# Modulation products in runs of two row tiles, spread by the columns of products done

## The chip, the core and the metric

The kernel runs on one core of one Trainium2 chip. The metric is device time of that core in microseconds, for one execution of the whole network. All operands are in HBM at the start; the output goes back there.

## The reference, cut to what matters

Two blocks follow each other on 256 tokens of width 1024. The first has four layers with two streams, latent tokens (256) and context tokens (256); the second has one layer with three attentions, a merge and a gated MLP, on the latent tokens alone. The change touches the first block only:

```python
def modulation(cvec, w_ada, b_ada):              # cvec: 1024; w_ada: 1024 x 3072
    return jnp.split(jax.nn.silu(cvec) @ w_ada + b_ada, 3, axis=-1)

for i in range(4):                               # mixers: window GQA, MLA, mLSTM, window GQA
    sh_l, sc_l, gt_l = modulation(c, w_ada, b_ada)
    sh_c, sc_c, gt_c = modulation(c_ctx, w_ada, b_ada)
    h_l = rmsnorm(x_lat, g_pre) * (1 + sc_l) + sh_l
    h_c = rmsnorm(x_ctx, g_pre) * (1 + sc_c) + sh_c
    y_l, y_c = mixer(h_l, h_c)                   # h @ w_in, attention, ... @ w_out
    x_lat = x_lat + gt_l * rmsnorm(y_l, g_post)
    x_ctx = x_ctx + gt_c * rmsnorm(y_c, g_post)  # not in the last layer
```

A layer's modulation depends on `c` and `c_ctx` only, so it can be computed at any time ahead of its use: shift and scale when the layer's input is normalised, the gate when its output is added.

## The kernel before

**Products.** An fp32 operand is held as two halves, high (`wh`, `thl`, ...) and low (`wl`, `tll`, ...), and every large product is three matmuls over them (`gemm_a`, L366 to L368, 512 columns at a time; `gemm_b`, L377 to L380, 256 columns). The weights come in parts of 512 KB (`load_part`): SP issues a DMA into one of three buffers `wr`, ScalarE makes the high half (L345) and VectorE the low half (L347).

**Modulation.** `c` and `c_ctx` stand side by side as two of 32 columns of `cs`. A block is 1024 of the 3072 output columns: block 0 and block 1 hold half the scale and half the shift each, block 2 the gate. One row tile is 128 rows of `w_ada` by the 1024 columns of a block, 512 KB, in one of two buffers `ar`; eight row tiles make a block. Per row tile four products (L518), one for each 256 columns, go to four groups of 32 columns of the array and to four groups of 32 partitions of one PSUM tile; in fp32 each is two instructions, so a row tile is eight. A block holds its PSUM tile, one of three of the tag `tp`, from its first product to its last. Then the columns are evacuated (L535), transposed (L712) and turned into the next layer's scale and shift, or, for the gate, multiplied and written to DRAM, from where they are read back across the partitions. Layer 0's own shift and scale are made ahead of everything by `ada_first` (L490).

**What is done when.** While layer l runs, its own gate (block 2) and layer l+1's blocks 0 and 1 are due: 24 row tiles in layers 0, 1 and 2, and 8 in layer 3. They are steps of a generator, `self.filler`: one step loads one row tile and multiplies it. The generator is stepped by `load_part`, once behind each weight part that is loaded (`pump(rate)`, L339; not in layer 0's first two input blocks), and run to a given point by `drain`: up to the gate ahead of the output projection, and to its end behind each stream of the output projection (L648). With about as many weight parts as row tiles in a layer, some steps are left to the output projection, whose eight parts pump too.

```python
            raw = self.raw(src, off, kc * n)
            self.pump(rate)
```

**Order.** The program is written in one order and the Tile scheduler makes each engine's queue from it: of the instructions that it believes ready it takes the one that stands first in the program. TensorE, ScalarE, VectorE and SP then take their queues strictly in order on the chip, so an instruction that the scheduler put too early holds all behind it. By this the products of later parts of the program stand between the steps of an attention (`tp` transposes at L910 and L1110, exponentials at L889, products with the values at L915 and L1118 to L1120), and eight instructions of one row tile need not stand together. The loads of `ar` wait on SP until the product that reads the buffer last is done, with the loads of `wr` behind them.

**Attention and banks.** PSUM tags have these banks: `mm` three (products), `S` two (scores), `tp` three (transposes, attention outputs, modulation). In `gqa` (layers 0 and 3) an attention output holds one `tp` bank over two heads' groups while the transposed probabilities of each key tile go through another and are copied out by ScalarE or VectorE in turn (L704, L708); layer 0 has 48 such groups of four transposes, 24 in each of its two calls of `attend`.

Of the kernel before, what the change touches and what calls it, by code (L numbers as in the profile page):

```python
# [19 lines left out]
F32 = mybir.dt.float32  # L20
# [3 lines left out]
AF = mybir.ActivationFunctionType  # L24
OP = mybir.AluOpType
# [7 lines left out]
WSZ = 512 * KS  # L33
NRAW = 3
NADA = 2
RATE = 1
NW = 5
NMID = 4
SLOTS = {"wfh": 2, "wfl": 2, "K8": 2, "Z4": 4, "Q4": 4, "P4": 4, "T2": 3, "V4": 1}
# [58 lines left out]
WEIGHTS = {}  # L98
# [170 lines left out]
class Net:  # L269
    def __init__(self, tc, A, out, stack, upto=99):  # L270
        self.tc, self.nc, self.A, self.out = tc, tc.nc, A, out
        self.upto = upto
        P = lambda name, bufs, **k: stack.enter_context(tc.tile_pool(name=name, bufs=bufs, **k))
        self.const = P("const", 1)
        self.res = P("res", 1)
        self.wp = P("wp", 2)
        self.tmp = P("tmp", 2)
        self.ps = P("ps", 2, space=PSUM)
        self.dram = P("dram", 1, space=bass.MemoryType.DRAM)
        self.open("act")  # L280
        self.flip = 0
        self.deep = 0
        self.filler = iter(())
        self.later = None
        self.n = 0

# [39 lines left out]
        return self.act.tile(shape, dt, name=self.nm(name), tag=name, bufs=1)  # L326


    def load(self, name, b, tags=None, rate=RATE):

        return [self.load_part(name, b, i, tags, rate) for i in range(len(WEIGHTS[name].off[b]))]

    def load_part(self, name, b, i, tags=None, rate=RATE):
        nc, w = self.nc, WEIGHTS[name]
        src = self.A["w_" + name]
        if True:
            off, k0, kc, n = w.off[b][i]
            raw = self.raw(src, off, kc * n)
            self.pump(rate)  # L339
            if tags is None:  # L340
                hi = self.wp.tile([128, WSZ], F32R, name=self.nm("wh"), tag="w", bufs=2 * NW)
                lo = self.wp.tile([128, WSZ], F32R, name=self.nm("wl"), tag="w", bufs=2 * NW)
            else:
                hi, lo = (self.t([128, WSZ], F32R, t) for t in tags)
            nc.scalar.activation(hi[:, :kc * n], raw[:, :kc * n], AF.Copy)  # L345
# [13 lines left out]
    def gemm_a(self, ps, xh, xl, parts, KC=8, n0=0, n=None):  # L359

        n = n or ps.shape[-1]
        nc = self.nc
        for k0, kc, wh, wl in parts:
            for k in range(kc):
                kk = k0 + k
                nc.tensor.matmul(ps, xh(kk), wh[:, k, n0:n0 + n], start=kk == 0, stop=False)  # L366
                nc.tensor.matmul(ps, xh(kk), wl[:, k, n0:n0 + n], start=False, stop=False)  # L367
                nc.tensor.matmul(ps, xl(kk), wh[:, k, n0:n0 + n], start=False, stop=kk == KC - 1)  # L368

    def gemm_b(self, outs, parts, n0, KC=8, m=128):  # L370

        nc = self.nc
        for k0, kc, wh, wl in parts:
            for k in range(kc):
                kk = k0 + k
                for ps, xh, xl in outs:
                    nc.tensor.matmul(ps, wh[:, k, n0:n0 + m], xh(kk), start=kk == 0, stop=False)  # L377
                    nc.tensor.matmul(ps, wh[:, k, n0:n0 + m], xl(kk), start=False, stop=False)  # L378
                for ps, xh, xl in outs:
                    nc.tensor.matmul(ps, wl[:, k, n0:n0 + m], xh(kk), start=False, stop=kk == KC - 1)  # L380


    def dma(self, out, in_):
# [79 lines left out]
                "l": l, "bcol": bcol, "gpre": gpre,  # L463
                "g": self.dram.tile([2, D], F32, name=f"gate{l}")}

    def pump(self, n):
        for _ in range(n):
            if next(self.filler, None) is None:
                break

    def drain(self, upto=None):

        for v in self.filler:
            if upto is not None and v == upto:
                break

    def ada_first(self, mod, g):
# [24 lines left out]
            nc.vector.tensor_mul(mod["A"][v][:, ks], t, gpre[:, ks])  # L502
            nc.vector.tensor_add(mod["B"][v][:, ks], tp[:, 2:4, j], bcol[:, ks])

    def ada_steps(self, mod, pairs):


        nc, A = self.nc, self.A
        l, bcol, gpre = mod["l"], mod["bcol"], mod["gpre"]
        w = WEIGHTS[f"l{l}_ada"]  # L510
        src = A[f"w_l{l}_ada"]
        for b in pairs:
            ps = self.pt([128, 256], "tp")
            for off, k, kc, n in w.off[0 if l == 0 else b]:
                r = self.wp.tile([128, 1024], F32, name=self.nm("ar"), tag="ar", bufs=NADA)
                self.dma(r, bass.AP(tensor=src.tensor, offset=src.offset + off, ap=[[n, 128], [1, n]]))
                for g in range(4):
                    nc.tensor.matmul(ps[32 * g:32 * g + 32, :], self.cs[:, k, :], r[:, g * 256:(g + 1) * 256],  # L518
                                     start=k == 0, stop=k == 7)
                yield "part"  # L520
            rows = self.mid([128, 256])
            if b == 2:
                br = self.tmp.tile([128, 2, 256], F32, name=self.nm("br"), tag="big", bufs=2)
                for i, t in enumerate(("brow", "gpost")):
                    for g in range(4):
                        self.dma(br[32 * g:32 * g + 32, i], bass.AP(tensor=A[f"l{l}_{t}"].tensor,
                                                                    offset=A[f"l{l}_{t}"].offset + g * 256,
                                                                    ap=[[0, 32], [1, 256]]))
                nc.vector.tensor_add(rows, ps, br[:, 0])
                nc.vector.tensor_mul(rows, rows, br[:, 1])  # L530
                for g in range(4):
                    self.dma(mod["g"][:, g * 256:(g + 1) * 256], rows[32 * g:32 * g + 2, :])
                yield "gate"
                continue
            nc.scalar.activation(rows, ps, AF.Copy)  # L535
            tp = self.pt([128, 2, 128], "tp")
            self.transposes(tp, rows, 2)
            cp = tp.rearrange("p j (h g v) -> p h g j v", h=2, g=2)
            pair = lambda x: x.rearrange("p (g j) -> p g j", g=2)
            k0 = b * 4  # L540
            for i, v in enumerate("lc"):
                t = self.tmp.tile([128, 4], F32, name=self.nm("sc"), tag="sc", bufs=2)
                nc.vector.scalar_tensor_tensor(pair(t), cp[:, 0, :, :, i], 1.0, pair(bcol[:, 8 + k0:12 + k0]),
                                               op0=OP.add, op1=OP.add)
                nc.vector.tensor_mul(mod["A"][v][:, k0:k0 + 4], t, gpre[:, k0:k0 + 4])
                nc.vector.tensor_add(pair(mod["B"][v][:, k0:k0 + 4]), cp[:, 1, :, :, i], pair(bcol[:, k0:k0 + 4]))

    def ada_all(self, mod, nxt):
        yield from self.ada_steps(mod, (2,))
        if nxt is not None:  # L550
            yield from self.ada_steps(nxt, (0, 1))

    def gates(self, mod, streams):

# [220 lines left out]
    def gqa(self, l, hT, mod, nxt, need_ctx, p0):  # L775
# [68 lines left out]
            return lambda q, i, b: lq[q][:, i, b, :]  # L844

        p0 = p0 or self.load(name, 0)
        p1 = self.load(name, 1, ("Z4", "P4"), rate=0 if l == 0 else RATE)
        q0 = {}
        if l == 0:
            for s, q, tag in (("c", 0, "mm"), ("c", 1, "mm"), ("l", 0, "mm"), ("l", 1, "S")):  # L850
# [80 lines left out]
            for g, z in enumerate((z0, z1)):  # L931
                self.split(y, g, z, qstreams)
        if need_ctx:
            self.drain("gate")
        else:
            self.drain()
            self.constants()
# [4 lines left out]
    def mla(self, hT, mod, nxt):  # L942
# [192 lines left out]
        y = self.halves("cl")  # L1135
        for g in range(2):
            self.split(y, g, z[g], "cl")
        self.drain("gate")
        self.mark("out1")
        return self.out_proj("l1_out", "cl", y, mod, nxt)  # L1140

# [1 line left out]
    def mlstm(self, hT, mod, nxt):  # L1143
# [233 lines left out]
        self.drain("gate")  # L1377
        self.mark("out2")
        return self.out_proj("l2_out", "lc", y, mod, nxt)

# [579 lines left out]
    def run(self):  # L1960
# [8 lines left out]
        for g in range(4):  # L1969
            self.ada_first(mod, g)  # L1970
            self.turn(hT["c"], xn["c"], *AB["c"], (g,))
            p0.append(self.load_part("l0_in", 0, g, None, 0))
# [55 lines left out]
```

## Time and profile before

| what | us |
|---|---|
| median of 3 runs | 1478.16 (1475.01 to 1479.94) |
| the profiled execution, its own time | 1472.61 |
| its span, first to last instruction | 1470.8 |
| TensorE matmul busy | 1433.8 (97% of the span) |
| TensorE weight load busy | 1171.0 (80%) |
| VectorE busy | 1046.3 (71%) |
| ScalarE busy | 737.2 (50%) |
| mean granted TensorE clock | 0.996 of full speed |

The four layers of the first block take roughly the first 960 us, the second block the rest. PE is the matmul side of TensorE, PEld its weight loads, DVE VectorE, ACT ScalarE, SP the engine that issues the DMAs. Matmuls overlap in the array, so the duration of one (0.28 us for 256 columns) is longer than the distance to the next.

### The profile page before, as it was taken

The numbers are of one execution on the slowest core, as the hardware profiler recorded it, in microseconds if no ns is written. First come the engines' busy times: TensorE is split into PE (matmuls) and PEld (weight loads), VectorE is DVE, ScalarE is ACT, GpSimd is POOL, SyncE is SP. The second block draws the span as 40 slices with busy tenths as digits, with TensorE's granted clock in tenths as the row PEclk, the third lists the DMA queues.
The fourth block names the chain that finished last, engine by engine and source line by source line (L and its number), as shares of the span: only waits on it lengthen the run. The fifth ranks groups of instructions, "written<-read, shape, count | busy, mean of one in ns | idle before, by whom it ended". The sixth has DMA issues, their size and how long they took to land.

```text
span 1470.8 us, 24541 instructions
## 1 busy us (share of the span) xinstructions
PE 1433.8 (97%) x9445; PEld 1171.0 (80%) x9445; DVE 1046.3 (71%) x2241; ACT 737.2 (50%) x1447; POOL 50.3 (3%) x72
## 2 busy tenths in 40 slices
PE   7999999999899999999999999999999999899998
PEld 4876677779687777787878777768988899799987
DVE  4678765553687666696585768889787887799963
ACT  4555543442456344364544535656575645466542
POOL 0000000000000000010000000000000000211100
PEclk9999999999999999999999999999999999999999
DMA  9601315552313325424323332246524444555552
GB/s 364 199 1 58 115 63 202 202 193 94 122 44 110 134 72 179 158 72 163 110 101 115 128 131 100 88 127 216 176 98 158 154 133 134 182 186 186 183 178 98
DMA packets 63555, 203.35 MB, mean 138 GB/s; under 512 B 10329, under 2 KB 14542, under 8 KB 63438
## 3 DMA queue, kind: packets, MB, share of 16 engines
q1 hardware_dynamic: 63438, 201.79, 40.8%
q8 instruction: 74, 1.21, 0.3%
q14 instruction: 43, 0.35, 0.1%
HBM read 200.65 MB, written 1.11 MB: 137 GB/s over the span
## 4 chain that ended last, share of the span: by engine, by line
PE 86%; DMA 5%; DVE 5%; ACT 2%; issue 1%; POOL 0%; SPq 0%; ACTq 0%; DVEq 0%; POOLq 0%
PE mm L366 11%; PE mm L368 11%; PE mm L367 11%; PE mm L377 8%; PE mm L378 7%; PE mm L380 7%; DMA ar<-in_w_l_ada_dram 3%; PE tp L518 3%; PE tp L915 3%; PE tp L910 3%; PE tp L712 2%; PE S L876 1%; PE S L380 1%; PE S L377 1%; PE S L378 1%
## 5 line engine op out<-in xcount | busy, mean ns | idle before, releaser
L347 DVE TENSOR_TENSOR wl<-wr,wh 128x1024 fp32r<-128x1024 f32 (+5 forms) x168 | 196.9, 1181 | 68.5 <-ACT wh L345 66.0
L345 ACT ACTIVATE wh<-wr 128x1024 fp32r<-128x1024 f32 (+5 forms) x172 | 174.6, 1026 | 90.6 <-PE mm L378 32.8
L377 PE MATMUL mm<-thl,wh 128*128 128x256 f32 x608 | 175.3, 289 | 1.3 <-ACT thl L661 1.3
L378 PE MATMUL mm<-tll,wh 128*128 128x256 f32 x608 | 173.5, 286 | 0.0
L380 PE MATMUL mm<-thl,wl 128*128 128x256 f32 x608 | 173.2, 286 | 0.0
L366 PE MATMUL mm<-wh,thl 128*128 128x512 f32 (+3 forms) x312 | 122.6, 393 | 1.4 <-ACT thl L661 1.0
L367 PE MATMUL mm<-wl,thl 128*128 128x512 f32 (+3 forms) x312 | 122.2, 392 | 0.0
L368 PE MATMUL mm<-wh,tll 128*128 128x512 f32 (+3 forms) x312 | 122.2, 392 | 0.0
L377 PEld LDWEIGHTS mm<-thl,wh 128*128 128x128 f32 x608 | 116.2, 191 | 4.2 <-issue 1.9
L378 PEld LDWEIGHTS mm<-tll,wh 128*128 128x128 f32 x608 | 116.3, 191 | 1.6 <-issue 1.2
L380 PEld LDWEIGHTS mm<-thl,wl 128*128 128x128 f32 x608 | 116.0, 191 | 0.7 <-issue 0.3
L368 PE MATMUL mm<-wh,tlc 128*128 128x512 f32 (+2 forms) x240 | 94.0, 394 | 0.3 <-DVE tlc L1886 0.3
L366 PE MATMUL mm<-wh,thc 128*128 128x512 f32 (+2 forms) x232 | 92.6, 399 | 1.6 <-DVE thc L595 1.6
L367 PE MATMUL mm<-wl,thc 128*128 128x512 f32 (+2 forms) x232 | 91.1, 394 | 0.0
L347 DVE TENSOR_TENSOR wl<-wrd,wh 128x1024 fp32r<-128x1024 f32 x52 | 65.9, 1269 | 27.5 <-ACT wh L345 27.4
L889 ACT ACTIVATE P<-S,nm 128x512 f32<-128x512 f32 (+1 forms) x96 | 58.6, 614 | 53.3 <-DVE nm L882 45.4
L366 PEld LDWEIGHTS mm<-wh,thl 128*128 128x128 f32 x312 | 58.7, 188 | 13.0 <-issue 1.6
L368 PEld LDWEIGHTS mm<-wh,tll 128*128 128x128 f32 x312 | 58.7, 188 | 10.8 <-issue 1.0
L345 ACT ACTIVATE wh<-wrd 128x1024 fp32r<-128x1024 f32 x52 | 53.6, 1050 | 26.6 <-PE mm L367 23.7
L367 PEld LDWEIGHTS mm<-wl,thl 128*128 128x128 f32 x312 | 58.7, 188 | 10.0 <-issue 0.8
L377 PE MATMUL mm<-thc,wh 128*128 128x256 f32 (+1 forms) x216 | 65.5, 303 | 0.1
L380 PE MATMUL mm<-thc,wl 128*128 128x256 f32 (+1 forms) x216 | 64.8, 300 | 0.0
(564 smaller groups left out, 3744.9 us busy)
## 6 DMA issues: line engine op xcount, KB each, us to landing
ar<-in_w_l_ada_dram SPq DMA_DIRECT2D x80, 512.0 KB
wr<-in_w_l_in_dram SPq DMA_DIRECT2D x48, 512.0 KB
wr<-in_w_l_out_dram SPq DMA_DIRECT2D x32, 512.0 KB
wr<-in_w_s_mg_dram SPq DMA_DIRECT2D x24, 512.0 KB
wrd<-in_w_s_down_dram SPq DMA_DIRECT2D x22, 512.0 KB
wrd<-in_w_s_gate_dram SPq DMA_DIRECT2D x20, 512.0 KB
wrd<-in_w_s_up_dram SPq DMA_DIRECT2D x20, 512.0 KB
wr<-in_w_s_br_dram SPq DMA_DIRECT2D x12, 512.0 KB
```

The costliest lines, as they stand in the source:

```text
L345: nc.scalar.activation(hi[:, :kc * n], raw[:, :kc * n], AF.Copy)
L347: eng.tensor_sub(lo[:, :kc * n], raw[:, :kc * n], hi[:, :kc * n].bitcast(F32))
L366: nc.tensor.matmul(ps, xh(kk), wh[:, k, n0:n0 + n], start=kk == 0, stop=False)
L367: nc.tensor.matmul(ps, xh(kk), wl[:, k, n0:n0 + n], start=False, stop=False)
L368: nc.tensor.matmul(ps, xl(kk), wh[:, k, n0:n0 + n], start=False, stop=kk == KC - 1)
L377: nc.tensor.matmul(ps, wh[:, k, n0:n0 + m], xh(kk), start=kk == 0, stop=False)
L378: nc.tensor.matmul(ps, wh[:, k, n0:n0 + m], xl(kk), start=False, stop=False)
L380: nc.tensor.matmul(ps, wl[:, k, n0:n0 + m], xh(kk), start=False, stop=kk == KC - 1)
L518: nc.tensor.matmul(ps[32 * g:32 * g + 32, :], self.cs[:, k, :], r[:, g * 256:(g + 1) * 256], start=k == 0, stop=k == 7)
L889: nc.scalar.activation(p[:, :nk], ps[:, i, :], AF.Exp, scale=scale, bias=nm[:, r:r + 1], accum_out=sm[:, r:r + 1])
L910: nc.tensor.transpose(tp[:, r, :], P[r][:, j * 128:(j + 1) * 128], self.eye)
L915: nc.tensor.matmul(o[i * 64:(i + 1) * 64, kv], vv, pT[:, 2 * i:2 * i + 2, :], start=j == 0, stop=j == nj - 1)
```

## The change

Three things change together. A step of the generator now takes two row tiles: it first sends the product of the pair that the step before has fetched, and then fetches the next pair into the two buffers; the first pair of a layer is fetched at the layer's start. The sixteen instructions of a pair are sent as one run: the first waits for the tile fetched last, and the others are tied to stand behind it in TensorE's queue, with high priority. And the generator is no longer stepped by weight parts, but by `earn`: each `gemm_a` or `gemm_b` adds the columns it has sent to a credit, and when the credit reaches the layer's pace (19000, 16000, 29000, 24000 columns) one step is taken. `drain(mod)` steps until the gate is done. By these columns the twelve steps of layers 0 to 2 end ahead of the output projection, at some 233,000 of 344,000 columns in layer 0, 194,000 of 301,000 in layer 1 and 356,000 of 492,000 in layer 2; the four of layer 3 end at 98,000. Shapes, loads and arithmetic stay what they are; the two row tiles of a pair are added in the other order.

```diff
-RATE = 1
+PACE = (19000, 16000, 29000, 24000)
...
+        self.pace = self.credit = 0
...
     def load_part(self, name, b, i, tags=None):
             raw = self.raw(src, off, kc * n)
-            self.pump(rate)
...
     def gemm_a(...)
+        self.earn(3 * n * sum(p[1] for p in parts))
...
     def gemm_b(...)
+        self.earn(sum(3 * o[0].shape[-1] for o in outs) * sum(p[1] for p in parts))
+
+    def earn(self, columns):
+        self.credit += columns
+        if self.credit >= self.pace > 0:
+            self.credit -= self.pace
+            next(self.filler, None)
...
-    def pump(self, n):
-        for _ in range(n):
+    def drain(self, gate=None):
+        for _ in iter(lambda: gate is not None and "done" in gate, True):
             if next(self.filler, None) is None:
-                break
-
-    def drain(self, upto=None):
-        for v in self.filler:
-            if upto is not None and v == upto:
                 break
...
-    def ada_steps(self, mod, pairs):
-        for b in pairs:
-            ps = self.pt([128, 256], "tp")
-            for off, k, kc, n in w.off[0 if l == 0 else b]:
-                r = self.wp.tile([128, 1024], F32, name=self.nm("ar"), tag="ar", bufs=NADA)
-                self.dma(r, bass.AP(tensor=src.tensor, offset=src.offset + off, ap=[[n, 128], [1, n]]))
-                for g in range(4):
-                    nc.tensor.matmul(ps[32 * g:32 * g + 32, :], self.cs[:, k, :], r[:, g * 256:(g + 1) * 256],
-                                     start=k == 0, stop=k == 7)
-                yield "part"
+    def ada_steps(self, blocks):
+        todo = None
+        for mod, b in blocks:
+            l = mod["l"]
+            parts = WEIGHTS[f"l{l}_ada"].off[0 if l == 0 else b]
+            src = A[f"w_l{l}_ada"]
+            for i in range(0, len(parts), NADA):
+                if todo is not None:
+                    self.ada_product(*todo)
+                rows = []
+                for off, k, kc, n in parts[i:i + NADA]:
+                    r = self.wp.tile([128, 1024], F32, name=self.nm("ar"), tag="ar", bufs=NADA)
+                    self.dma(r, bass.AP(tensor=src.tensor, offset=src.offset + off, ap=[[n, 128], [1, n]]))
+                    rows.insert(0, (k, r))
+                todo = (mod, b, rows)
+                yield True
+        self.ada_product(*todo)
+        yield True
+
+    def ada_product(self, mod, b, rows):
+        k0 = min(k for k, _ in rows)
+        if k0 == 0:
+            mod["ps"] = self.pt([128, 256], "tp")
+        ps = mod["ps"]
+        def part(i, g):
+            k, r = rows[i]
+            return self.nc.tensor.matmul(ps[32 * g:32 * g + 32, :], self.cs[:, k, :], r[:, g * 256:(g + 1) * 256],
+                                         start=k0 == 0 and i == 0, stop=k0 + NADA == 8 and i == NADA - 1)
+        self.together([(lambda i=i, g=g: part(i, g)) for i in range(NADA) for g in range(4)])
+        if k0 + NADA == 8:
+            (self.ada_gate if b == 2 else self.ada_columns)(mod, b, ps)
+
+    def together(self, work):
+        first = work[0]()
+        with self.tc.issue_after(first.ins), self.tc.high_priority():
+            for w in work[1:]:
+                w()
...
-        p1 = self.load(name, 1, ("Z4", "P4"), rate=0 if l == 0 else RATE)
+        p1 = self.load(name, 1, ("Z4", "P4"))
...
-            self.filler = self.ada_all(mod, nxt)
+            self.filler = self.ada_steps([(mod, 2)] + ([(nxt, 0), (nxt, 1)] if nxt is not None else []))
+            self.pace, self.credit = PACE[l], 0
+            next(self.filler)
```

`ada_gate` and `ada_columns` hold the former code for a finished block, moved and otherwise unchanged; `ada_gate` marks the gate as done.

## Rows read from the trace of the kernel before

**Rows 1.** The page's busy shares: busy us, share of the span, instructions.

```profile
PE 1433.8 (97%) x9445; PEld 1171.0 (80%) x9445; DVE 1046.3 (71%) x2241; ACT 737.2 (50%) x1447; POOL 50.3 (3%) x72
```

**Rows 2.** Table by stretches: length, busy us of engines, clock, DMA share, GB/s.

```profile
145.00:215.00 70.00, 69.94 (x512) 47.30 (x510) 49.51 (x128) 35.57 (x94) 0.00 (x0) 1.00 0.23 77
215.00:240.00 25.00, 24.22 (x211) 22.90 (x210) 10.90 (x15) 6.68 (x8) 0.00 (x0) 1.00 0.46 166
382.00:384.00 2.00, 2.00 (x11) 0.99 (x12) 1.36 (x5) 0.00 (x0) 0.00 (x0) 0.50 0.13 52
```

**Rows 3.** Instructions grouped by line, L518: busy us, mean ns, idle before, releaser.

```profile
L518 PE MATMUL tp<-ar,cs 128*32 128x256 f32 x640 | 57.3, 398 | 7.1 <-DMA ar<-in_w_l_ada_dram 7.0
```

**Rows 4.** Timeline of PE around a run of 8: start us, duration us, instruction.

```profile
247.46 0.40 PE L366 MATMUL mm<-wh,thc 128*128 128x512 f32 x1
247.70 0.39 PE L367 MATMUL mm<-wl,thc 128*128 128x512 f32 x1
248.01 0.64 PE L518 MATMUL tp<-ar,cs 128*32 128x256 f32 x8
248.58 0.50 PE L368 MATMUL mm<-wh,tlc 128*128 128x512 f32 x1
248.92 0.39 PE L366 MATMUL mm<-wh,thc 128*128 128x512 f32 x1
```

**Rows 5.** Timeline of PE around a run of 16.

```profile
240.02 0.28 PE L378 MATMUL mm<-tll,wh 128*128 128x256 f32 x1
240.14 0.28 PE L380 MATMUL mm<-thl,wl 128*128 128x256 f32 x1
240.35 1.07 PE L518 MATMUL tp<-ar,cs 128*32 128x256 f32 x16
241.35 0.50 PE L366 MATMUL mm<-wh,thc 128*128 128x512 f32 x1
```

**Rows 6.** Waits of PE: waiter, releaser, us in total, times, longest us.

```profile
PE tp L518 <- DMA ar<-in_w_l_ada_dram: 7.0, 8, 2.8
```

**Rows 7.** Timeline of PE, the first and the last run of L518.

```profile
145.54 0.62 PE L518 MATMUL tp<-ar,cs 128*32 128x256 f32 x2
...
854.85 0.64 PE L518 MATMUL tp<-ar,cs 128*32 128x256 f32 x8
```

**Rows 8.** Timeline of PE, the run of 16 in layer 2's start.

```profile
588.07 1.94 PE L518 MATMUL tp<-ar,cs 128*32 128x256 f32 x16
```

**Rows 9.** Chain of waits, two pieces: start us, us from issue to landing.

```profile
375.65 6.18 DMA ar<-in_w_l_ada_dram
...
848.23 4.64 DMA ar<-in_w_l_ada_dram
```

**Rows 10.** Timeline of PE behind the longest wait for a row tile.

```profile
381.88 1.08 PE L518 MATMUL tp<-ar,cs 128*32 128x256 f32 x8 [2.79 <-DMA ar<-in_w_l_ada_dram]
...
383.91 0.63 PE L380 MATMUL mm<-thc,wl 128*128 128x512 f32 x1
384.34 0.63 PE L377 MATMUL mm<-thc,wh 128*128 128x512 f32 x1
```

**Rows 11.** Table by stretches, PE alone: L1110 (two rows), then tile ar (two).

```profile
405.00:444.00 39.00, 6.76 (x43) 1.00 0.14 41
444.00:483.00 39.00, 6.25 (x40) 1.00 0.43 148
...
383.00:490.00 107.00, 10.47 (x80) 0.97 0.31 104
444.00:483.00 39.00, 6.10 (x56) 1.00 0.43 148
```

**Rows 12.** Instructions grouped by line, L708, copies of transposed probabilities.

```profile
L708 DVE COPY T<-tp 128x512 f32<-128x512 f32 x40 | 27.6, 690 | 18.5 <-PE tp L910 10.8 <-PE S L880 7.3
```

More of the change, by code (lines that the diff above doesn't have):

```diff
@@ L326, in k, with load, load_part @@
         return self.act.tile(shape, dt, name=self.nm(name), tag=name, bufs=1)
-    def load(self, name, b, tags=None, rate=RATE):
-        return [self.load_part(name, b, i, tags, rate) for i in range(len(WEIGHTS[name].off[b]))]
-    def load_part(self, name, b, i, tags=None, rate=RATE):
+    def load(self, name, b, tags=None):
+        return [self.load_part(name, b, i, tags) for i in range(len(WEIGHTS[name].off[b]))]
+    def load_part(self, name, b, i, tags=None):
         nc, w = self.nc, WEIGHTS[name]
@@ L503, in ada_first @@
             nc.vector.tensor_add(mod["B"][v][:, ks], tp[:, 2:4, j], bcol[:, ks])
-    def ada_steps(self, mod, pairs):
+    def ada_steps(self, blocks):
         nc, A = self.nc, self.A
-        l, bcol, gpre = mod["l"], mod["bcol"], mod["gpre"]
-        w = WEIGHTS[f"l{l}_ada"]
-        src = A[f"w_l{l}_ada"]
-        for b in pairs:
-            ps = self.pt([128, 256], "tp")
-            for off, k, kc, n in w.off[0 if l == 0 else b]:
-                r = self.wp.tile([128, 1024], F32, name=self.nm("ar"), tag="ar", bufs=NADA)
-                self.dma(r, bass.AP(tensor=src.tensor, offset=src.offset + off, ap=[[n, 128], [1, n]]))
-                for g in range(4):
-                    nc.tensor.matmul(ps[32 * g:32 * g + 32, :], self.cs[:, k, :], r[:, g * 256:(g + 1) * 256],
-                                     start=k == 0, stop=k == 7)
-                yield "part"
[L521 to L551, printed above, removed]
+        todo = None
[13 more added lines that the diff above has]
+                yield True
@@ new lines, in together, with ada_gate @@
+    def together(self, work):
[3 more added lines that the diff above has]
+                w()
+    def ada_gate(self, mod, b, ps):
+        nc, A, l = self.nc, self.A, mod["l"]
+        rows = self.mid([128, 256])
+        br = self.tmp.tile([128, 2, 256], F32, name=self.nm("br"), tag="big", bufs=2)
+        for i, t in enumerate(("brow", "gpost")):
+            for g in range(4):
+                self.dma(br[32 * g:32 * g + 32, i], bass.AP(tensor=A[f"l{l}_{t}"].tensor,
+                                                            offset=A[f"l{l}_{t}"].offset + g * 256,
+                                                            ap=[[0, 32], [1, 256]]))
+        nc.vector.tensor_add(rows, ps, br[:, 0])
+        nc.vector.tensor_mul(rows, rows, br[:, 1])
+        for g in range(4):
+            self.dma(mod["g"][:, g * 256:(g + 1) * 256], rows[32 * g:32 * g + 2, :])
+        mod["done"] = True
@@ new lines, in ada_columns @@
+    def ada_columns(self, mod, b, ps):
+        nc, bcol, gpre = self.nc, mod["bcol"], mod["gpre"]
+        rows = self.mid([128, 256])
+        nc.scalar.activation(rows, ps, AF.Copy)
+        tp = self.pt([128, 2, 128], "tp")
+        self.transposes(tp, rows, 2)
+        cp = tp.rearrange("p j (h g v) -> p h g j v", h=2, g=2)
+        pair = lambda x: x.rearrange("p (g j) -> p g j", g=2)
+        k0 = b * 4
+        for i, v in enumerate("lc"):
+            t = self.tmp.tile([128, 4], F32, name=self.nm("sc"), tag="sc", bufs=2)
+            nc.vector.scalar_tensor_tensor(pair(t), cp[:, 0, :, :, i], 1.0, pair(bcol[:, 8 + k0:12 + k0]),
+                                           op0=OP.add, op1=OP.add)
+            nc.vector.tensor_mul(mod["A"][v][:, k0:k0 + 4], t, gpre[:, k0:k0 + 4])
+            nc.vector.tensor_add(pair(mod["B"][v][:, k0:k0 + 4]), cp[:, 1, :, :, i], pair(bcol[:, k0:k0 + 4]))
@@ L933, in gqa @@
         if need_ctx:
-            self.drain("gate")
+            self.drain(mod)
         else:
@@ L1137, in mla @@
             self.split(y, g, z[g], "cl")
-        self.drain("gate")
+        self.drain(mod)
         self.mark("out1")
@@ L1376, in mlstm @@
             y[s] = self.turn(self.halves(s)[s], [O[s, 0], O[s, 1]], gh)
-        self.drain("gate")
+        self.drain(mod)
         self.mark("out2")
@@ L1971, in run @@
             self.turn(hT["c"], xn["c"], *AB["c"], (g,))
[L1972 removed]
+            p0.append(self.load_part("l0_in", 0, g))
             if g == 0:
```

## Prediction

> **What bounds the kernel now.** I read the page's busy shares first, then the table by stretches, then the modulation matmuls (line 518) in the timeline, and last who waits for their tiles. TensorE matmul is busy for 97% of the span [rows 1], and the stretch 215 to 240 us shows that this is no empty figure: 24.22 of 25 us [rows 2], with a new 256-column matmul every 0.12 us [rows 5]. So time taken off TensorE's queue there comes off the end. The stretch 145 to 215 us is softer: matmul is busy for 69.94 of 70 us, but weight load only for 47.30 [rows 2].
>
> The modulation's 640 instructions (80 row tiles, 8 each) are busy for 57.3 us, and TensorE stands 7.0 us before them waiting for their tiles [rows 3], in 8 waits [rows 6]. I counted their runs in the timeline: 78, of 2 to 16 instructions (45 of 8, 8 of 16, 25 split), first at 145.54 us, last at 854.85 us [rows 7].
>
> **The change, part by part.** Durations are those of the profiled execution: 1472.6 us, a span of 1470.8 and 1.8 around it. The median shown, 1478.2, lies 5.5 above; I take the sum off it unchanged.
>
> *Fewer, longer runs.* A run of 8 between 512-column matmuls: from the matmul at 247.70 to the second one behind the run, at 248.92, are 1.22 us [rows 4]. Two undisturbed steps would take 2 x 0.24 (247.46 to 247.70), so the run costs 0.74 to 0.76 us; it is shown busy for 0.64, so some 0.12 lies beside the busy time. A run of 16: 240.14 to 241.35 is 1.21 us [rows 5], less 0.12 for the matmul ahead, plus the 0.1 by which the first matmul behind a run is slow (0.34 for 0.24 in rows 4): 1.20 us, again its 1.07 busy and 0.12 more. Even a run of 2 is busy for 0.62 [rows 7]. So before: 57.3 + 78 x 0.12 = 66.7 us. After: 40 pairs of 16 instructions, kept together, 40 x 1.20 = 48.0 us. Of the difference of 18.7 I drop 0.9 us: the run at 588.07 took 1.94 instead of 1.07 [rows 8] behind a stall that is not the modulation's, and whatever comes there next will be as slow. Another 0.4 belongs to the clock term below. **Gain 17.4 us.** The bounds are 0 (the runs stay as split as now) and 18.7.
>
> *Waits for tiles.* The present 7.0 us go: they fall where a run of two tiles has just freed both buffers and the next tile is wanted soon (landing 4.64 to 6.18 us after issue [rows 9]). **Gain 7.0.**
>
> *Clock.* The longest wait, 2.79 us, ends at 381.88. The granted clock of 382 to 384 us is 0.50, which is 1.2 GHz [rows 2], the run of 8 is busy 1.08 instead of 0.64, and 512-column matmuls start 0.43 us apart (383.91, 384.34) instead of 0.24 [rows 10]; five such steps lose 5 x 0.19. **Gain 1.4** with the run's own 0.4. Gross: 17.4 + 7.0 + 1.4 = 25.8 us.
>
> *Cover that goes.* In layer 1's attention the modulation partly fills holes. The transposes of line 1110 mark its progress: 43 in the 39 us from 405, with no modulation, and 40 in the 39 us from 444, with 56 modulation instructions, 6.10 us busy [rows 11]. Nine runs there cost 6.1 + 9 x 0.12 = 7.2 us of queue but held the attention up by 3 transposes, 3 x 39/43 = 2.7 us: 0.37 of their cost. From 383 to 490 us there are 16 runs, 10.47 us busy [rows 11], 12.4 with their ends. Four pairs of the new plan fall there, 4.8 us. Of the 7.6 us between, 63% are not gained. **Loss 4.8.** Bounds: 0, and 7.6.
>
> *New waits.* A step now sends one product and at once fetches the next pair into the two buffers just freed, so a pair has one step to land. By the code's column counts and 0.12 us per 256 columns, steps lie 5.0 to 17.3 us apart; the paces 19000 and 16000 are 8.9 and 7.5 us. Six steps, two in layer 0 and four in layer 1, have only 5.0 to 5.8 us of products between them, against 4.64 to 6.18 for the first tile of two [rows 9], the second somewhat later. The scheduler puts other matmuls ahead of a product that it believes late, but TensorE takes its queue in order, so all behind a late pair waits. I take six waits of 0.5 us. **Loss 3.0.** Bounds: 0, and 24 waits (all pairs of layers 0 and 1) at today's mean of 7.0/8 = 0.87 [rows 6], 20.9 us.
>
> *Moved DMAs.* All 80 ada loads stay on SP's queue. Two of layer 0 now stand ahead of the second input block's loads, behind which ScalarE, VectorE and then the queries wait. I cost this at nothing: that block's conversions come after the present first modulation load at 45 us, and TensorE has the key and value products until then. Without that cover it is about two landings in sequence, no more than 2 x 6.18 us, and no less than 0. The gate's row loads and the gate's write come earlier and have no reader before the output projection; nothing is gained or lost by them. Evacuations, transposes and column arithmetic are the same in number: 0.
>
> *A PSUM bank.* The accumulator of a block holds one of three tp banks through its four steps. In layer 0, steps 5 to 8 straddle both attentions in program order, so transposes there have one bank less beside the output's. Layer 1's two halves answer this as far as the trace can: from 444 us a modulation block holds a bank, from 405 none does, and the 2.7 us above contain that difference. So 0 beyond the cover term. Upper bound: the 48 groups of four transposes in layer 0 each wait for a copy out of the bank, 0.69 us [rows 12], 33 us; below 0 nothing, since holding a bank gives none back.
>
> Net: 25.8 - 4.8 - 3.0 = 18.0 us, so 1472.6 - 18.0 = 1454.6 by the profile, **1460** by the median.
>
> **Rivals.**
>
> *All of it (12%).* No pair is late and attention finds other cover: 1478.2 - 25.8 = 1452. For it: layer 0's attention has 25 us of plain products left over behind it (215 to 240 us). Against: rows 11.
>
> *Busy is not bound (17%).* In the attention stretches freed matmul time only turns into idle time, as weight load at 47.30 of 70 us suggests [rows 2]. Then the 9 runs of 145 to 215 us (6.53 busy, 7.6 in all) and the 12.4 of 383 to 490 count nothing: 65.4 - 7.6 - 12.4 = 45.4 us of runs outside, replaced by 36 pairs at 1.20 = 43.2, for four stay inside. Gain 2.2 + 7.0 + 1.4 - 3.0 = 7.6: 1471. Against it: plain products wait to be drawn forward after 215 us.
> The Trainium skill, "Trainium Kernel Development and Optimization", section "Best Practices", says to judge the distance from the limit by the weight load's busy share and not by the matmul's. By that rule the 97% proves little (weight load 80%, rows 1), and this rival would hold; rows 5 support my reading only for plain products.
>
> *Late pairs (8%).* With both buffers freed by one run, every pair of layers 0 and 1 is awaited: 20.9 us instead of 3.0, gain 0.1, **1478**: no change. For it: rows 9 against steps of 5 to 8.9 us; against: 70 of 78 runs now wait for nothing.
> The Trainium skill, "TensorE: Matmul & The Clock Gate", section "HAM oscillation", warns that waiting for a transfer between short groups of matmuls drops the clock at every group. Here the wait of 2.79 us did so (rows 10); each such wait would add 1.4 us.
>
> *Slower: the starved transposes (6%).* The bank held in layer 0 is short, the scheduler runs out of products to put between, and TensorE idles 0.69 us at each of 48 transpose groups: 33 us lost, 1460 + 33 = 1493. It decides against the change from 27 uncovered groups (18.0/0.69).
>
> *Pairs don't stay together (5%).* If the order behind the first instruction is not kept and 78 runs remain, only waits and clock go: 7.0 + 1.4 - 3.0 = 5.4, 1473.
>
> **How the numbers follow.** My forecast has 52%, and 1453 to 1467 as its own range (new waits from 0 to 6, cover lost from 0 to 7.6). The range 1447 to 1474 takes in the full gain less the 5 us by which runs of one kernel differ, and the attention rival; it leaves out late pairs, starved transposes and half of the unkept pairs, with the tails. A measurement of this kernel tells 0.3% (4.4 us) from nothing. Faster than 1473.7: the forecast, the full gain, most of the attention rival, part of the unkept pairs, 82%. Within: late pairs and the rest of those two, 10%. Slower: starved transposes and a little of late pairs, 8%.
>
> **What would show it.** Right: 40 runs of 16 (1.07 us busy) in the timeline, the busy time of these instructions near 43 us, waits for ar tiles near 3 us and none above 1.5, full clock at layer 1's start. The cover term: more idle TensorE between 395 and 490 us than now. Wrong: many short waits for ar tiles in layers 0 and 1; transposes of layer 0 waiting for copies out of PSUM; runs still split; or TensorE's idle time growing by as much as its busy time falls.

## The result and the profile after

The changed kernel takes 1456.69 us, median of 4 runs (1453.88 to 1458.74), beside 1476.59 for the kernel before on the same chip: a ratio of 0.9865, 95% interval 0.9832 to 0.9898. Forecast were 1460 (1447 to 1474) and faster with 82%. The profiled execution took 1455.3 us, 17.3 less than the one of before, against 18.0 in the sum.

First the page's busy shares of the kernel after (busy us, share of the span, instructions), which answer to [rows 1].

```profile
PE 1418.6 (98%) x9445; PEld 1172.7 (81%) x9445; DVE 1044.2 (72%) x2241; ACT 736.0 (51%) x1447; POOL 51.5 (4%) x72
```

The span of 1453.5 us is 17.3 shorter. TensorE is busy for 15.2 us less; its idle time (span less busy) went from 37.0 to 34.9. Next the modulation's group of instructions after (line 540 of the changed kernel is what line 518 was), for [rows 3], and the first and the last of its runs in the timeline, for [rows 7].

```profile
L540 PE MATMUL tp<-ar,cs 128*32 128x256 f32 x640 | 42.8, 385 | 0.0
```

```profile
50.04 1.07 PE L540 MATMUL tp<-ar,cs 128*32 128x256 f32 x16
...
301.53 0.36 PE L368 MATMUL mm<-wh,tlc 128*128 128x448 f32 x1
301.82 1.07 PE L540 MATMUL tp<-ar,cs 128*32 128x256 f32 x16
302.82 0.39 PE L378 MATMUL mm<-thc,Q 128*128 128x256 f32 x1
303.04 0.28 PE L379 MATMUL mm<-tlc,Q 128*128 128x256 f32 x1
...
878.91 1.07 PE L540 MATMUL tp<-ar,cs 128*32 128x256 f32 x16
```

All 40 pairs go as one run of 16, busy for 42.8 us together (57.3 before), and no product waits for its tile (7.0 us before). The middle rows give a pair's price between plain products: from 301.53 to 303.04 are 1.51 us, less one 448-column step of 0.20 (300.51 to 300.71 further up) and one 256-column step of 0.12: 1.19 us. The sum had 1.20.

TensorE's waits after (waiter, releaser, us in total, times, longest us), for [rows 6]; rows that stand much alike before are left out.

```profile
PE tp L618 <- DVE xn L606: 2.3, 4, 1.3
...
PE S L908 <- ACT P L921: 1.4, 1, 1.4
```

There is no row for `ar`. What stands in its place is small and spread: the transposes of the normalised input wait 2.3 us for VectorE (0.7 before), the scores of layer 3 wait 1.4 for one exponential (nothing of note before). Added over all lines, TensorE's other idle time grew by 5.0 us, while the modulation's fell by 7.1.

To see where the time was won I compared when the two kernels reach the same point of the work (after minus before, us; the first matmul of that kind in each timeline):

| point | before at | after |
|---|---|---|
| layer 0: first product with the values | 87.9 | +6.9 |
| layer 0: last such product | 214.5 | -2.1 |
| layer 1: first input product | 298.5 | -6.5 |
| layer 1: first, last product with the values | 403.3, 494.2 | -9.4, -13.4 |
| layer 2: gate; last product with the values | 563.9, 760.5 | -16.3, -22.5 |
| layer 3: first, last product with the values | 898.3, 983.1 | -25.6, -22.1 |
| second block: first input product | 998.4 | -18.0 |
| second block: first scores of `ka`, last matmul | 1060.4, 1466.6 | -17.5, -17.3 |

Layer 0's modulation now begins at 50 us and not at 145, so at the first point the new kernel has done five pairs more (50.04 to 84.69), 5 x 1.20 = 6.0 us. By these marks layers 0 to 2 win about 22 us, and layer 3 and the seam behind it give some 5 back.

The marks follow one kind of matmul each, so work that one kernel draws forward and the other puts off looks like a loss or a lead. From layer 2's last product with the values to the end, TensorE has this left to do, before and after (length, busy us and number of instructions, clock, DMA share, GB/s):

```profile
760.54:1470.80 710.26, 698.50 (x4543) 1.00 0.44 146
```

```profile
738.01:1453.50 715.49, 702.51 (x4568) 1.00 0.45 147
```

The changed kernel has 25 instructions more ahead of it, a pair (at 747.16) and nine plain ones, some 3 us of work. So its lead there is nearer 19 us than 22, and what goes back behind it is nearer 2 us than 5.

### The profile page after: what moved, and what is told of

The parts are those of the page before. It is cut to its first block, busy times and chain, and to the rows that moved or that the text cites. A ratio compares the mean times of both kernels' runs of the same rounds, so it can differ in the third digit from the quotient of the medians.

```text
span 1453.5 us, 24554 instructions
## 1 busy us (share of the span) xinstructions
PE 1418.6 (98%) x9445; PEld 1172.7 (81%) x9445; DVE 1044.2 (72%) x2241; ACT 736.0 (51%) x1447; POOL 51.5 (4%) x72
## 4 chain that ended last, share of the span: by engine, by line
PE 82%; DVE 8%; ACT 4%; issue 3%; DMA 2%; POOL 0%; SPq 0%; ACTq 0%; DVEq 0%; POOLq 0%
PE mm L366 10%; PE mm L368 10%; PE mm L367 10%; PE mm L378 8%; PE mm L381 8%; PE mm L379 8%; PE tp L947 3%; PE tp L942 3%; PE tp L540 2%; PE tp L744 2%; PE S L378 1%; PE S L379 1%; PE S L381 1%; PE S L908 1%; DVE wl L347 1%
## 5 line engine op out<-in xcount | busy, mean ns | idle before, releaser
L367 PE MATMUL mm<-wl,thc 128*128 128x512 f32 (+2 forms) x232 | 90.9, 393 | 0.0
L368 PEld LDWEIGHTS mm<-wh,tll 128*128 128x128 f32 x312 | 58.7, 188 | 10.8 <-issue 0.6
```

## The experiments

Each ratio is to the kernel before, run in the same set on the same chip. There were three sets, in which the kernel before took 1473.0, 1474.2 and 1474.4 us, so times of different sets can be compared to within 1.5 us. A trace is one execution, and its time is not the median. The changed kernel run again in the first set:

> The changed kernel again, timed beside the others of this set. All theories: 0.984 to 0.989 of the kernel before, 40 runs of sixteen instructions and no wait for a row tile.

Measured: 1456.29 us, ratio 0.9880 [0.9861, 0.9899], span 1453.9; 40 runs of 16, waits for tiles 1.7 us (two, longest 1.2). So the saving is there again, and the absence of waits in the first trace is not exact: 0 to 1.7 us from one execution to the next.

**The tie taken away.** The order behind the first instruction and the high priority go together:

```diff
         first = work[0]()
-        with self.tc.issue_after(first.ins), self.tc.high_priority():
-            for w in work[1:]:
-                w()
+        for w in work[1:]:
+            w()
```

> The pairs and the spreading stay, only the tie behind the first instruction and the high priority go. If runs matter (each further run costs some 0.3 us of TensorE's queue: 2 x 0.75 for two of eight against 1.20 for one of sixteen) and the scheduler splits them as it did before (25 of 78 were split), 50 to 65 runs appear and the kernel is 3 to 8 us slower than the changed one. If the pairs stay together anyway, because both tiles have long landed, there are 40 to 45 runs and the time is the same within 2 us.

Measured: 1465.19 us, 0.9937 [0.9917, 0.9958], a little more than the 3 to 8 us expected. Nine pairs come apart, eight of them in an attention or at its edge and one among layer 2's input products (546 us): 54 runs. The timeline of TensorE of the untied kernel in layer 0's attention:

```profile
103.11 0.62 PE L540 MATMUL tp<-ar,cs 128*32 128x256 f32 x2
103.66 0.50 PE L907 MATMUL S<-K,Q 128*128 128x512 f32 x1
...
106.83 0.64 PE L540 MATMUL tp<-ar,cs 128*32 128x256 f32 x8
107.40 0.55 PE L941 MATMUL tp<-eye,P 128*128 128x128 f32 x3
107.88 0.63 PE L540 MATMUL tp<-ar,cs 128*32 128x256 f32 x6
108.44 0.33 PE L941 MATMUL tp<-eye,P 128*128 128x128 f32 x1
```

and its group of modulation instructions:

```profile
L540 PE MATMUL tp<-ar,cs 128*32 128x256 f32 x640 | 49.8, 386 | 3.9 <-DMA ar<-in_w_l_ada_dram 2.4 <-DVE P L1128 1.4
```

By the prediction's price, busy time and 0.12 us a run, that is 49.8 + 54 x 0.12 = 56.3 us against 42.8 + 40 x 0.12 = 47.6: 8.7 more, and 2.2 more of idle time before them than in the repeated kernel (3.9 against its 1.7), 10.9 in all. Measured are 8.9 by the medians (1465.19 - 1456.29) and 13.8 between the two executions with a trace (1469.50 - 1455.68), of which the untied one was the slowest of its six. By the marks layer 0's attention alone ends 5.4 us later (+3.3 for -2.1), with three pairs in eight runs there. So a piece costs about its price even inside an attention. The rival that freed matmul time turns into idle time there falls for these pairs.

**Single tiles, spread alike.** One row tile a step, at half the pace, in two buffers, tied to runs of 8:

```diff
-NADA = 2
-PACE = (19000, 16000, 29000, 24000)
+NADA = 1
+PACE = (9500, 8000, 14500, 12000)
...
-    r = self.wp.tile([128, 1024], F32, name=self.nm("ar"), tag="ar", bufs=NADA)
+    r = self.wp.tile([128, 1024], F32, name=self.nm("ar"), tag="ar", bufs=2)
```

> One row tile to a run, tied, half the pace, two buffers as before, each tile fetched one step ahead: 80 runs of eight instead of 40 of sixteen. If a run's fixed cost is on the path, 80 x 0.75 = 60 us stand for 48: 10 to 13 us slower than the changed kernel, with no waits for tiles, so only 6 to 8 us faster than the kernel before. If matmul busy is not the bound in the attentions, less than 6 us slower.

Measured: 1472.71 us, 0.9988 [0.9975, 1.0000]. The modulation's group in it:

```profile
L540 PE MATMUL tp<-ar,cs 128*32 128x256 f32 x640 | 50.9, 391 | 3.7 <-DMA ar<-in_w_l_ada_dram 3.7
```

The timeline has 79 runs, for two tiles happen to follow each other: 50.9 + 79 x 0.12 = 60.4, which is 12.8 over the pairs, and 2.0 more of waits than in the repeated kernel: 14.8 us. Measured are 16.4, where 10 to 13 and no waits were expected. The kernel was also expected 6 to 8 us faster than the one before; it is 0.3 us faster by the medians (1473.00 - 1472.71). The spread without the pairs brings nothing that a measurement can tell.

**Pairs not spread.** All paces doubled, so that about half of a layer's pairs are left to the output projection, where `drain` sends them:

```diff
-PACE = (19000, 16000, 29000, 24000)
+PACE = (38000, 32000, 58000, 48000)
```

> The changed kernel with each pace doubled (38000, 32000, 58000, 48000 columns), so that only about half of the pairs of a layer are sent before its output projection and the rest are sent there, one behind the other, by the calls of drain: 40 runs of 16 as in the changed kernel, but not spread. Theory (a run's cost is fixed and fully on the path, and what the pairs need is a step that is long enough for the transfers): the runs stay at 47 to 48 us, but in each of layers 0 to 2 some six pairs follow each other with nothing between but the projection's products, and a pair needs two transfers of 512 KB, 4.64 us and more each; 4 of 6 pairs late by 1 to 3 us in three layers are 12 to 36 us of waits for tiles, ratio 0.995 to 1.01. Rival (the scheduler draws products of the next layer between, so the spread is worth nothing): waits below 3 us, ratio 0.986 to 0.990 as the changed kernel.

Measured: 1478.11 us, 1.0024 [1.0009, 1.0040]: the runs are still 40 of 16, and the whole gain is gone. The waits of TensorE in this kernel:

```profile
PE mm L366 <- DVE yg L664: 8.8, 3, 3.6
...
PE tp L540 <- DMA ar<-in_w_l_ada_dram: 7.8, 4, 4.0
```

The tiles cost 7.8 us of waits, under the 12 to 36 expected. As much (the 8.8 for `yg`) is lost where I had expected nothing, at the seams between layers. TensorE's timeline at the seam from layer 0 to layer 1:

```profile
286.85 1.07 PE L540 MATMUL tp<-ar,cs 128*32 128x256 f32 x16 [1.95 <-DMA ar<-in_w_l_ada_dram]
288.42 0.44 PE L744 MATMUL tp<-eye,mid 128*128 128x128 f32 x2 [0.51 <-ACT mid L572]
288.69 1.48 PE L618 MATMUL tp<-eye,xn 128*128 128x128 f32 x12
290.41 0.66 PE L618 MATMUL tp<-eye,xn 128*128 128x128 f32 x4 [0.23 <-ACT mid L625]
294.65 0.80 PE L366 MATMUL mm<-Q,thl 128*128 128x512 f32 x1 [3.59 <-DVE yg L664]
295.25 0.63 PE L367 MATMUL mm<-P,thl 128*128 128x512 f32 x1
295.68 0.63 PE L368 MATMUL mm<-Q,tll 128*128 128x512 f32 x1
```

and VectorE's in the same stretch:

```profile
289.17 0.15 DVE L580 SCALAR_TENSOR_TENSOR sc<-tp,bcol 128x4 f32<-128x4 f32 x1
...
290.38 0.43 DVE L627 CAST thc<-mid 128x512 fp32r<-128x512 f32 x1 [0.86 <-ACT mid L625]
290.84 0.69 DVE L628 TENSOR_TENSOR tlc<-mid,thc 128x512 fp32r<-128x512 f32 x1
...
293.92 0.68 DVE L664 TENSOR_TENSOR yg<-mm,K 128x512 f32<-128x512 f32 x1
```

The last pair of layer 0 ends at 288 us; only then are the next layer's scale and shift made (289.17). The whole normalised input of one stream follows in one piece on VectorE, ahead of the `yg` that reads a product out of PSUM, and the output projection's next product waits 3.59 us for the bank that `yg` empties. Behind that wait the steps between 512-column matmuls are 0.43 us instead of 0.23. The lower clock is a third loss; behind the long waits of this kernel lie these stretches (length, busy us of PE, clock, DMA share, GB/s):

```profile
294.00:300.00 6.00, 5.34 (x13) 0.50 0.00 0
823.00:829.00 6.00, 4.17 (x27) 0.50 0.43 137
833.00:839.00 6.00, 5.27 (x12) 0.50 0.06 12
```

Their 14.8 us of matmuls at half speed cost some 7 us, an estimate. The step from the last product of layer 0's attention to layer 1's input is 15.4 us longer than in the changed kernel by the table's marks (from -6.6 to +4.4, against -2.1 to -6.5); 4.8 of this are four pairs more that fall into it, eight for four. So the products of a layer's row tiles are due well ahead of the end of its output projection.

**Half the pace.** The opposite, all steps early:

```diff
-PACE = (19000, 16000, 29000, 24000)
+PACE = (9500, 8000, 14500, 12000)
```

> Half the paces (9500, 8000, 14500, 12000): in layers 0 and 1 a step comes every 4 to 5.8 us of products, less than the 4.6 to 6.2 us in which the first tile of a pair landed. If late pairs cost, waits for tiles grow from 0 to 1.7 us to 10 or more and the kernel is 5 to 15 us slower than the changed one. If the scheduler holds the products back by itself, waits stay under 4 us and the time is the same within 4 us.

Measured: 1469.83 us, 0.9970 [0.9950, 0.9989]. Its timeline of TensorE at the longest wait, and the clock there (length, busy us of PE, PEld, DVE, ACT and POOL, clock, DMA share, GB/s):

```profile
100.16 1.94 PE L540 MATMUL tp<-ar,cs 128*32 128x256 f32 x16 [3.89 <-DMA ar<-in_w_l_ada_dram]
...
107.96 1.94 PE L540 MATMUL tp<-ar,cs 128*32 128x256 f32 x16
```

```profile
100.00:102.00 2.00, 1.84 (x16) 0.59 (x16) 0.00 (x0) 0.00 (x0) 0.00 (x0) 0.50 0.00 0
```

There are six waits, 7.6 us, between the two expectations (10 or more, and under 4); the time is that of the late pairs. Layer 0's first product with the values comes 25.1 us later than before, where the changed kernel is 6.9 late, and layer 1 begins 3.3 late instead of 6.5 early. This is the late-pairs rival, at half the distance of the pairs: 9.8 of the 13.5 us lost (1469.83 - 1456.29) are lost in layer 0. The granted clock behind the wait is 0.50, the level of 1.2 GHz, and each of the two pairs there takes 1.94 us. The Trainium skill, "TensorE: Matmul & The Clock Gate", section "HAM oscillation", warns that waits for transfers between groups of matmuls bring the clock down; this row agrees, and the changed kernel's trace, which has no wait for a tile, keeps 1.00 from 374 to 478 us, where [rows 2] had 0.50 for a while.

**Fetch in the same step.**

```diff
     rows.insert(0, (k, r))
-    todo = (mod, b, rows)
+    self.ada_product(mod, b, rows)
     yield True
```

(with the product of the former step and the fetch at the layer's start taken out)

> Each pair is fetched in the step that sends its product, not one step ahead; the paces stay. A pair lands 5 to 7 us after its issue. If TensorE's queue is ordered for that by the scheduler, the products simply move some 6 us later among other work, waits for tiles stay under 5 us in all and the kernel is within 4 us of the changed one. If the step ahead is what removes the waits, 40 pairs wait 0.5 to 1 us each: 20 to 40 us slower.

Measured: 1459.34 us, 0.9897 [0.9865, 0.9930], waits for tiles 1.3 us in three. Fetching a step ahead in program order is worth some 3 us by the medians, and the intervals overlap: with waits no larger than in the repeated kernel (1.7 us), the scheduler itself puts the products behind the transfers.

**The bank.** The accumulator in the tag `mm` instead of `tp`:

```diff
-            mod["ps"] = self.pt([128, 256], "tp")
+            mod["ps"] = self.pt([128, 256], "mm")
```

> The blocks' accumulators lie in a bank of the tag mm instead of tp, so the attentions keep all three tp banks. If a bank held through the attentions starves the transposes, time comes back: 5 us or more faster than the changed kernel. If it costs nothing (as layer 1's two halves in the kernel before suggest), the time is that of the changed kernel within 3 us, or some us more where products miss their third bank.

Measured: 1458.73 us, 0.9897 [0.9868, 0.9925]. Giving the transposes their third bank back wins nothing; layer 0's attention ends 6.6 us later by the marks (+4.5 for -2.1), so `mm` is no better a place.

**Layer 3.** Two theories for the 5 us that it gives back. One: the gate's read-back across partitions waits on SP for 22 us (925 to 948) with the output projection's weights behind it; so it was sent through GpSimd.

```diff
-        self.nc.sync.dma_start(out, bass.AP(...))
+        (self.nc.gpsimd if n == D else self.nc.sync).dma_start(out, bass.AP(...))
```

> The gate's read back across the partitions is issued by GpSimd instead of SP, where it waits 22 us in layer 3 and 45 us in another layer with weight loads behind it. If that block of SP's queue makes layer 3 give back 5 us of its lead (from 22.5 us ahead at the end of layer 2's attention to 17.4 at the end), they stay: 1450 to 1453 us. If the fourth pair in the attention makes the loss by itself, the time is that of the changed kernel within 2 us.

Measured: 1457.16 us, 0.9882 [0.9853, 0.9911]; layer 3 gives back as before (-19.9 ahead of layer 3, -14.1 in the second block). The theory falls. The other: a pair or the gate's work lies inside the attention.

```diff
-PACE = (19000, 16000, 29000, 24000)
+PACE = (19000, 16000, 29000, 12000)
```

> Layer 3's pace 12000 instead of 24000: its four pairs are sent before the first attention call. The changed kernel was 24.8 us ahead at 860 us of the old trace and only 17.4 ahead at the end; between, its TensorE idles in layer 3's attention. If the fourth pair and its bank inside the attention cause that, up to 7 us come back and the lead at the end is 22 to 25 us. If it is the order of SP's queue there (the gate's read back waits 22 us for a buffer with the output projection's weights behind it), the lead stays at 15 to 19 us.

Measured: 1453.30 us, 0.9862 [0.9841, 0.9882]; from layer 2's last product to the second block it gives back 1.2 us, not 5.0. Its lead at the end, 19.7 us by the medians (1473.00 - 1453.30), lies between the two ranges expected, 22 to 25 and 15 to 19. Table by stretches (columns as above), first the changed kernel, then this one:

```profile
915.00:935.00 20.00, 17.61 (x113) 12.25 (x112) 15.57 (x41) 10.26 (x27) 0.00 (x0) 1.00 0.25 82
```

```profile
915.00:935.00 20.00, 20.00 (x141) 15.46 (x140) 17.64 (x43) 12.74 (x30) 0.00 (x0) 1.00 0.22 73
```

The hole of 2.4 us in layer 3's attention is closed. This is the fastest kernel of the study. The intervals of the two ratios overlap, but its four times (1453.1 to 1453.5) all lie below the changed kernel's five on the same chip (1454.7 to 1457.0); the difference is 0.2%. With both edits, early pairs and the other bank:

> The changed kernel with two edits at once: layer 3's pace 12000 columns instead of 24000, so that its four pairs go before its attention, and the accumulators of the modulation in the PSUM tag mm instead of tp. Alone the first measured 0.9862 [0.9841, 0.9882] of the kernel before and the second 0.9897 [0.9868, 0.9925], the changed kernel 0.9880 [0.9861, 0.9899]. Theory (what layer 3 gives back comes from a pair inside its attention, and the bank that a block holds costs nothing): the span lies 18 to 20 us under that of before, as with the pace alone, and the wait of TensorE for ScalarE's exponentials near 918 us is absent. Rival (the bank is what the pair inside the attention takes away, so either edit removes the same loss and the bank also frees layer 0): 3 us or more faster than with the pace alone, 22 to 24 us under before.

Measured: 1458.12 us, 0.9892 [0.9868, 0.9916]: 16.3 us under the kernel before by the medians, 11.2 by the spans of the traces (this one's is from the slowest of four runs). So it is neither 18 to 20 nor 22 to 24, and both statements miss. The hole near 918 is absent, and so it is with the other bank alone at the old pace (20.00 of 20 us busy there, too). From layer 2 on, the kernels at 12000 columns give back 1.2 and 3.8 us and, at half pace, win 1.6; those at 24000 give back 1.8 to 6.3, the single tiles (the same columns for two tiles) 7.4, the doubled paces 18.1. That is a tendency, and the marks hold different amounts of work put off. Edits worth 3 us move the scheduler's order elsewhere by as much, and what layer 3 loses is not settled.

## Why the prediction came out right

**Fewer, longer runs (17.4).** The price of a run holds in each step: 40 runs of 1.07 us, 42.8 busy against 43, 1.19 us a pair for 1.20, and the untied and the single-tile kernel lie 8.9 and 16.4 us above the pairs where the price of a run gives 10.9 and 14.8 with their waits. That this time lies on the path also in attention was the point against "busy is not bound". The Trainium skill, "Trainium Kernel Development and Optimization", section "Best Practices", judges the distance from the limit by the weight load's busy share, beside the share of peak arithmetic, and not by the matmul's; the weight load's share is 80 to 81% in all these kernels and does not tell them apart.

Against the kernel before, the price does not come off the end in full. With busy time, ends and waits, it spends 66.7 + 7.0 = 73.7 us on these products, the single tiles 60.4 + 3.7 = 64.1, the untied pairs 56.3 + 3.9 = 60.2, the repeated changed kernel 47.6 + 1.7 = 49.3. That would be 9.6, 13.5 and 24.4 us won; the medians of that set give 0.3, 7.8 and 16.7. Some 6 to 9 us are missing in all three, however long their runs. That points to what the three share, the new places of the products, and not to the pairs, though no run takes it apart; the next terms say where it is lost, as far as that is known.

What the prediction did not see is a condition. Its sum has no term for the spread: nothing in it says that the pairs would lose their gain if they were not spread. Spread alone is worth 0.12% [0.00, 0.25], pairs alone (paces doubled) lose 0.24% [0.09, 0.40], and both together win 1.2% [1.0, 1.4]. Doubling the paces is not the stepping of before, by weight parts; pairs stepped by weight parts were not tried.

**Waits for tiles (7.0) and clock (1.4).** Both went; the clock from 374 to 478 us, where [rows 2] had 0.50 for a while, is 1.00 (the changed kernel's stretch, all engines):

```profile
374.00:478.00 104.00, 99.36 (x640) 80.66 (x641) 92.16 (x228) 63.77 (x147) 0.00 (x0) 1.00 0.30 97
```

The prediction looked at one stretch of low clock and left a second as it was (the 0.9 us at 588.07). Between its first 25 us and its last 5, the kernel before has three; the two that [rows 2] do not show are these (length, busy us of PE, clock, DMA share, GB/s):

```profile
399.00:402.00 3.00, 3.00 (x12) 0.50 0.00 0
587.00:590.00 3.00, 2.98 (x21) 0.50 0.03 8
```

The changed kernel has one, elsewhere; the repeated one has 1.00 there, too:

```profile
1261.00:1264.00 3.00, 3.00 (x16) 0.50 0.11 18
```

Three us at half speed lose 1.5, so two stretches fewer are up to 3 us where the sum had 1.4. Most of them follow waits that are not the modulation's, so part of that is chance.

**Cover that goes (4.8).** Between layer 1's first and last product with the values the kernel before has 64 modulation instructions, 7.36 us busy in 11 runs, 8.7 with their ends; the changed kernel has none, and the stretch shrinks from 90.9 to 86.9 us. So 4.0 are won and 4.7 are not, 54% of the cost. To this extent the rival that busy time is not bound in the attentions was right. The sum had four pairs in this attention; the last one starts at 392.82, ahead of it. That 4.7 comes so near to 4.8 is therefore chance: another share of another amount. The two stretches as a table, before and after:

```profile
403.30:494.20 90.90, 89.42 (x568) 71.05 (x569) 75.31 (x185) 52.68 (x119) 0.00 (x0) 1.00 0.31 104
```

```profile
393.90:480.80 86.90, 84.19 (x504) 69.58 (x505) 75.20 (x180) 52.80 (x119) 0.00 (x0) 1.00 0.23 74
```

Idle TensorE grows there as foretold, from 1.48 to 2.71 us, which is only a part of the 4.7; the rest is not seen as idle time. The working was weaker than its result: it laid the three transposes that came less in the second 39 us of [rows 11] to the modulation. The changed kernel, with no modulation in either half, also does fewer there (43, then 41), so two of the three have another reason:

```profile
395.00:434.00 39.00, 6.76 (x43) 1.00 0.19 65
434.00:473.00 39.00, 6.86 (x41) 1.00 0.21 63
```

**New waits (3.0).** Too high: 0 to 1.7 us. The step ahead is not what avoids them (fetching in the same step: 1.3 us); the distance of the steps is (half of it: 7.6 us and the clock).

**Moved DMAs and bank (0).** The bank is worth nothing measurable, as said. Ahead of layer 0's attention the moved loads are not seen at the given paces: of the +6.9 there, the five pairs done are 6.0. At half pace nine pairs done are 10.8 of the 25.1, and the lower clock and late tiles take part of the rest; whether moved loads do is not shown.

**What the sum lacked.** Layer 3. Four pairs at 1.20 instead of eight runs (5.5 us busy, 6.5 with their ends) should win 1.7 us there; instead 5 us go back by the marks between layer 2's last product and the second block, of which some 3 are work put off. That makes about 4 us less than the prices say, and why is not settled. The sum came out right in part by luck, because this and the waits that did not come lie on opposite sides: gross 25.8, less 4.7 of cover, less about 4 in layer 3, leaves 17, and 17.3 were measured. With the clock's share uncertain by 1.6 and the marks by more, that agreement is closer than the parts are known.

## What to carry to other kernels

Price a small tiled product by its runs, not by its instructions: count them in the timeline, and take the distance between the matmuls on both sides, not the busy time. Keeping a run together is worth its price only if the tiles arrive and the result is there ahead of its reader, so the place of each run (not later than the seam that needs it, not closer to the next than a transfer takes) counts as much as its length: at half and at double the paces most of the gain or all of it was gone. Before laying a slower stretch to one cause, look for a stretch without that cause that slows down as well.

## What the runs showed that I had not expected

A piece of 2, of 6 and of 8 modulation instructions holds TensorE for the same time: the next matmul starts 0.55, 0.56 and 0.57 us behind its start (103.11 to 103.66, 107.88 to 108.44 and 106.83 to 107.40 in the untied kernel), while 16 take 1.00 (301.82 to 302.82 in the changed one). So splitting a run of 8 into 2 and 6 costs as much as a second run of 8.

A wait of 1.95 us (286.85, paces doubled) left the run behind it at its 1.07 us; behind waits of 2.79, 3.59 and 3.89 us the steps were those of the lower clock. But the length of one wait does not decide it. These are TensorE's rows behind three other waits, the first in the kernel before, the others in the changed one:

```profile
398.56 0.50 PE L1078 MATMUL S<-Q,Q 128*128 128x512 f32 x1 [1.43 <-ACT P L1093]
```

```profile
569.63 0.66 PE L744 MATMUL tp<-eye,mid 128*128 128x128 f32 x4 [2.26 <-ACT mid L1254]
...
1260.01 0.66 PE L744 MATMUL tp<-eye,xl 128*128 128x128 f32 x4 [1.97 <-DVE xl L1928]
```

Behind the waits of 1.43 and 1.97 us the granted clock fell to 0.50 (399 to 402 and 1261 to 1264 us), behind the one of 2.26 us it stayed at 1.00 (569 to 573 us).
